# The list scheduler of a transformer layer plays on another simulation of the engines

## The chip, the core and the metric

The kernel runs on one core of a Trainium2 chip. The metric is the device time of one execution, in microseconds (us). Lower is better. The engines are named as the profile names them: PE is TensorE (matmuls; its weight loads are shown apart as PEld), DVE is VectorE, ACT is ScalarE, POOL is GpSimd and SP is SyncE, which here only issues DMAs.

## The reference

One layer of a transformer over 640 tokens of width 1024: 128 context tokens and 512 latent tokens on a grid of 8 rows by 64 columns. All values are fp32. Cut to what matters:

```python
sh1, sc1, g1, sh2, sc2, g2 = split(silu(c) @ w_mod + b_mod, 6)
h = rmsnorm(x, n1) * (1 + sc1) + sh1
aq, ak, av, bq, bk, bv, ga, gb = split(h @ w_in)              # 4352 columns
a_o = softmax attention, 8 query heads on 2 key heads; q and k normalised, 2-D rotary
b_o = neighbourhood attention, 8 heads, window of 8 x 16 grid places, learned bias
x = x + g1 * ((sigmoid(ga) * (a_o @ w_br_a) + sigmoid(gb) * (b_o @ w_br_b)) @ w_out)
h2 = rmsnorm(x, n2) * (1 + sc2) + sh2
x = x + g2 * (square(relu(h2 @ w_mlp_in)) @ w_mlp_out)        # 4096 hidden columns
y = rmsnorm(x, final_g)
```

Latent queries also read 128 cached context keys; context queries read context keys alone. The new keys and values of the context tokens are outputs too.

## The kernel before

**How the work is tiled.** Activations lie transposed, features on the 128 partitions and the 640 tokens along the free axis, in two halves of 320 columns. To keep the precision, each fp32 operand is cut into a high and a low part of the type fp32r: ACT copies the high part and DVE subtracts it to get the low part. Each product is then three matmuls (high by high, high by low, low by high), in `gemm_k` at L320 to L322 and, in the MLP, at L1679 to L1681.

**Its stages.**

1. The start, up to about 48 us: the modulation of the first norm, the first norm and the first three tiles of `w_in`, while the first loads arrive.
2. Attention, about 48 to 320 us. Units of work (`HeadA`, `HeadB`, `CtxPair`) go through scores (`S`: L700 and L701, or L763 and L764), a softmax (DVE maximum L702, ACT exponential L703), transposes (L710, L780), a cut into `ph` and `pl` (ACT L647, DVE L648), and the product with the values (L718 and L722). Between them the generator `fill_tile` gives out the matmuls of the other tiles of `w_in` (`pg`, L320 to L322), so many ns of them between two steps. On the program's side this mix of streams is written out: `attention` calls `F.spend` with what a step has left.
3. Merge, output projection and second norm, about 315 to 510 us. DVE also forms the late part of the modulation there (`wmt` times `cb`, L1123).
4. The MLP, to the end. Its first chunk is plain; from about 557 us on it is computed by a scheme of seven products of half-size blocks (the list `SEQ`, loop at L1665), each into one of eight PSUM banks `b`. Its weights come in as `wst` and `wsb` on SP's queue (L254, L1398). The `wsb` get a second matrix added by a DMA of POOL's queue that accumulates (L1401, L1424). ACT and DVE cut them into `wb` (L1416, L1421), of which six can be alive at once.
5. The tail: the last gated sums (L1532), squares (L1547), the mean by a matmul with ones (L1559), its power -1/2 (L1563, L1564), the final products (L1568) and the stores (L1569).

**What sets the order on the engines.** The Python code traces instructions in program order. When the tracing context closes, a list scheduler plays the program on a simulation of the chip: whenever an engine (or a DMA queue) can take an instruction, it is given the ready one with the best priority, and the priority is the place in program order (a few blocks are moved back or forward with `tc.high_priority(offset=...)`, as the weight cuts in attention by `DEFER` = 60). The order in which the simulation took the instructions becomes the order in each engine's stream. The chip then runs each stream strictly in that order. Buffers of a pool are also handed out at that moment, so which buffer a tile gets follows from the order.

Two stretches are kept in program order by hand. In the start all five engines are:

```python
with tc.manual_schedule(engines={e.engine for e in (PE, ACT, DVE, nc.gpsimd, nc.sync)}):   # L458
```

From the merge to the start of the MLP's first chunk, DVE alone is (L1170 with `MAN = (0,)`, closed at L1638). Everywhere else the simulation decides for all engines and both DMA queues.

## Time and profile before

| | |
|---|---|
| median of 3 runs | 917.35 us (917.27 to 917.84) |
| the profiled execution | 917.51 us, of which 915.7 us from its first to its last instruction |
| busy: PE, PEld | 901.5 us (98%), 871.5 us (95%) |
| busy: DVE, ACT, POOL | 713.5 us (78%), 564.8 us (62%), 197.0 us (22%) |
| bytes moved by DMA | 151.09 MB |
| instructions | 16620 |

A busy time is the sum of the stretches in which an engine ran at least one instruction. A matmul's end in the profile is modelled and matmuls overlap: two of 320 columns start 0.15 us apart in the dense stretches, and each is shown as 0.31 us long. So a PE that is shown busy all the time may still have lost time, which then shows as a longer mean of the matmuls that waited for their operands. Everything in this table but the median is of the one profiled execution.

### The profile page before, as it was taken

Reading aid. Unit: us, or ns where it says so; the run is one execution under the profiler, and the core shown is the slowest. Engines: PE = TensorE matmul, PEld = TensorE weight load, DVE = VectorE, ACT = ScalarE, POOL = GpSimd, SP = SyncE. Lnnn points to the kernel's source line nnn. Section 1 sums busy time; section 2 is a strip of 40 time slices with the busy share of each in tenths; the row PEclk is TensorE's granted clock in tenths of the full one; section 3 lists DMA queues with packets and bytes.
Section 4 is the critical chain, followed back from the end, with each engine's and each line's share of the span. In section 5 each row is a group of like instructions: output and inputs, shape, how many; then the busy total and the mean of one; then the engine's idle time right before and its main releaser. Section 6 shows DMA issues by size and latency. Waiting matters only on the chain.

```text
span 915.7 us, 16620 instructions
## 1 busy us (share of the span) xinstructions
PE 901.5 (98%) x6120; PEld 871.5 (95%) x6120; DVE 713.5 (78%) x1508; ACT 564.8 (62%) x1176; POOL 197.0 (22%) x226
## 2 busy tenths in 40 slices
PE   9999999999999999999999999999999999999996
PEld 7799989999999999999999999999999999999995
DVE  6776887757666796767789996995798769976897
ACT  4566777756667765765325667537753576357765
POOL 0020200001211011211120000354244532454140
PEclk9999999999999999999999999999999999999998
DMA  9892400126645398999743463898778876898475
GB/s 348 317 266 69 113 24 26 62 72 159 161 119 125 120 284 256 249 268 251 251 140 100 116 165 105 134 210 186 186 122 191 178 174 144 180 173 182 97 126 151
DMA packets 54465, 151.09 MB, mean 165 GB/s; under 512 B 6704, under 2 KB 10432, under 8 KB 54384
## 3 DMA queue, kind: packets, MB, share of 16 engines
q1 hardware_dynamic: 31440, 99.74, 33.1%
q0 software_dynamic: 21792, 48.98, 30.8%
q10 hardware_dynamic: 1152, 1.31, 0.4%
q8 instruction: 48, 0.79, 0.4%
q14 instruction: 33, 0.27, 0.1%
HBM read 137.67 MB, written 4.60 MB: 155 GB/s over the span
## 4 chain that ended last, share of the span: by engine, by line
PE 81%; DVE 6%; DMA 5%; ACT 4%; issue 2%; POOL 0%; SPq 0%; DVEq 0%; ACTq 0%; POOLq 0%
PE b L1680 10%; PE b L1679 10%; PE b L1681 10%; PE pg L320 7%; PE pg L321 7%; PE pg L322 7%; PE pss L322 4%; PE pss L321 4%; PE pss L320 4%; DMA wsb<-w 2%; PE pt L321 2%; PE pt L322 2%; PE pt L320 2%; DMA ms<-wmodA 2%; PE pt L710 1%
## 5 line engine op out<-in xcount | busy, mean ns | idle before, releaser
L1416 ACT ACTIVATE wb<-wsb 128x512 fp32r<-128x512 f32 x140 | 87.1, 628 | 90.6 <-PE b L1681 59.2
L1680 PE MATMUL b<-op,wb 128*128 128x320 f32 x448 | 138.6, 309 | 0.7 <-DVE op L1489 0.7
L1679 PE MATMUL b<-op,wb 128*128 128x320 f32 x448 | 138.6, 309 | 0.0
L1681 PE MATMUL b<-op,wb 128*128 128x320 f32 x448 | 138.4, 309 | 0.0
L1421 DVE TENSOR_TENSOR wb<-wsb,wb 128x512 fp32r<-128x512 f32 x124 | 92.5, 749 | 26.5 <-ACT wb L1416 26.3
L1424 POOL DMA_DIRECT2D wsb<-w x84 | 74.4, 922 | 127.8 <-DVE wb L1421 99.7
L1123 DVE SCALAR_TENSOR_TENSOR mt<-wmt,cb 128x512 f32<-128x512 f32 x128 | 80.9, 686 | 6.0 <-DMA wmt<-wmodB 6.0
L1680 PEld LDWEIGHTS b<-op,wb 128*128 128x128 f32 x448 | 84.1, 188 | 1.2 <-DVE op L1489 1.2
L1679 PEld LDWEIGHTS b<-op,wb 128*128 128x128 f32 x448 | 84.1, 188 | 0.5 <-DVE x L1532 0.4
L1681 PEld LDWEIGHTS b<-op,wb 128*128 128x128 f32 x448 | 84.1, 188 | 0.0
L272 ACT ACTIVATE wh<-wst 128x512 fp32r<-128x512 f32 (+1 forms) x84 | 61.1, 739 | 32.1 <-PE pg L321 16.6
L1401 POOL DMA_DIRECT2D wsb<-w x28 | 26.0, 930 | 138.0 <-DVE xm L341 41.5
L281 DVE TENSOR_TENSOR wl<-wst,wh 128x512 fp32r<-128x512 f32 (+1 forms) x53 | 43.3, 821 | 14.9 <-ACT wh L272 12.8
L648 DVE TENSOR_TENSOR pl<-pt,ph 128x512 fp32r<-128x512 f32 (+1 forms) x72 | 44.9, 627 | 11.8 <-ACT ph L647 11.2
L647 ACT ACTIVATE ph<-pt 128x512 fp32r<-128x512 f32 (+1 forms) x72 | 39.2, 548 | 15.7 <-PE po L718 4.7
L1532 DVE SCALAR_TENSOR_TENSOR x<-b,parts,x 128x128 f32<-128x128 f32 (+1 forms) x116 | 46.3, 429 | 2.9 <-PE b L1681 2.2
L1416 ACT ACTIVATE wb<-wst 128x512 fp32r<-128x512 f32 x56 | 34.9, 626 | 17.1 <-PE b L1681 10.3
L1679 PE MATMUL b<-t,wb 128*128 128x320 f32 x144 | 44.7, 310 | 0.0
L1681 PE MATMUL b<-t,wb 128*128 128x320 f32 x144 | 44.5, 309 | 0.0
L1680 PE MATMUL b<-t,wb 128*128 128x320 f32 x144 | 44.5, 309 | 0.0
L1489 DVE TENSOR_TENSOR op<-hid,op 128x1280 fp32r<-128x1280 f32 (+2 forms) x32 | 37.0, 1155 | 7.6 <-ACT op L1488 7.4
L1532 DVE SCALAR_TENSOR_TENSOR x<-tp,parts,x 128x320 f32<-128x320 f32 (+2 forms) x60 | 38.9, 677 | 1.0 <-ACT tp L1583 1.0
(890 smaller groups left out, 3009.2 us busy)
## 6 DMA issues: line engine op xcount, KB each, us to landing
wsb<-w POOLq DMA_DIRECT2D x112, 256.0 KB, 5.1
wst<-w SPq DMA_DIRECT2D x36, 512.0 KB, 3.9
wmt<-wmodB SPq DMA_DIRECT2D x32, 512.0 KB, 5.5
wst<-w_in SPq DMA_DIRECT2D x31, 512.0 KB, 4.4
wsb<-w SPq DMA_DIRECT2D x28, 512.0 KB, 4.0
ms<-wmodA SPq DMA_DIRECT2D x16, 512.0 KB, 8.2
wl<-w_in POOLq DMA_DIRECT2D x10, 512.0 KB, 7.6
wst<-w_br SPq DMA_DIRECT2D x8, 512.0 KB, 4.2
```

Of the source, the lines that this page charges most:

```text
L272: ACT.activation(hi[:, ks], st[:, ks], AF.Copy)
L320: PE.matmul(ps, wh[:, k], xh[:, sl], start=first, stop=False)
L321: PE.matmul(ps, wh[:, k], xl[:, sl], start=False, stop=False)
L322: PE.matmul(ps, wl[:, k], xh[:, sl], start=False, stop=last)
L1123: DVE.scalar_tensor_tensor(t, st[:, q * 512:(q + 1) * 512], 1.0, r32(cb[2 * q + i][:, :512]), op0=OP.mult, op1=OP.mult, accum_out=parts[:, ...
L1416: ACT.activation(w[:, 0:4], t, AF.Copy)
L1421: (nc.gpsimd if o in BLKPOOL[l - 1] else DVE).tensor_sub(w[:, 4:8], t, r32(w[:, 0:4]))
L1424: nc.gpsimd.dma_start(t, self.src(l, c, n, e)[:, 4 * half:4 * half + 4], accum_op=OP.add)
L1532: DVE.scalar_tensor_tensor(X1[i][:, sl], src[:, sl.start - off:sl.stop - off], g[:, j:j + 1], X1[i][:, sl], op0=OP.mult, op1=OP.add)
L1679: PE.matmul(b, w[:, k], xh, start=not whole and k == 0, stop=False, skip_group_check=True)
L1680: PE.matmul(b, w[:, k], xl, start=False, stop=False, skip_group_check=True)
L1681: PE.matmul(b, w[:, 4 + k], xh, start=False, stop=o not in ("A11", "S2", "S1") and k == 3, skip_group_check=True)
```

## The change

One argument of the tracing context. With it, the scheduler plays the program on a simulation that follows the devices of the core one by one: for each engine its sequencer, its queue of issued instructions and the engine itself, the PE's weight loads and matmuls apart, and the DMA queues and engines. Without it, the scheduler uses the library's default simulation, a coarser one. No instruction is added, removed or changed in shape; only orders in the streams, buffers and the semaphore waits that follow from them can differ.

```diff
-    with tile.TileContext(nc) as tc:
+    with tile.TileContext(nc, schedule_with_timeline_sim=True) as tc:
         trunk_layer(tc, *args)
```

## The prediction

> **What bounds the kernel now.** I read the head of the page first, then busy time by stage, then what PE waited for, then the groups of matmuls, then the other engines' waits and the chain that ended last.

> The head of the page says who leads: PE is busy nearly all the span and has most of the chain.

> ```profile
> span 915.7 us, 16620 instructions
> PE 901.5 (98%) x6120; PEld 871.5 (95%) x6120; DVE 713.5 (78%) x1508; ACT 564.8 (62%) x1176; POOL 197.0 (22%) x226
> PE 81%; DVE 6%; DMA 5%; ACT 4%; issue 2%; POOL 0%; SPq 0%; DVEq 0%; ACTq 0%; POOLq 0%
> ```

> The windows by stage (start, attention, merge to second norm, MLP, tail) show where PE lost anything. In each row: the stage, its length, then busy time and count for PE, PEld, DVE, ACT and POOL, the granted clock, the DMA share.

> ```profile
> 0.00:48.00 48.00, 46.22 (x354) 36.38 (x355) 33.20 (x91) 25.32 (x54) 1.74 (x6) 1.00 0.91 331
> 48.00:320.00 272.00, 268.56 (x1799) 252.66 (x1798) 195.45 (x425) 188.30 (x468) 33.94 (x53) 1.00 0.40 108
> 320.00:510.00 190.00, 189.88 (x1289) 188.83 (x1287) 147.46 (x412) 101.50 (x192) 27.24 (x27) 1.00 0.76 221
> 510.00:900.00 390.00, 389.29 (x2640) 387.25 (x2640) 326.76 (x560) 242.29 (x449) 134.06 (x140) 1.00 0.74 157
> 900.00:916.00 16.00, 7.58 (x45) 6.40 (x44) 10.65 (x25) 7.44 (x17) 0.00 (x0) 0.85 0.47 164
> ```

> PE's idle time is 1.78 us in the start, 3.44 in attention, 0.12 from merge to norm, 0.71 in the MLP, and 8.1 in the tail (15.7 - 7.58). So 580 us of the kernel, from 320 to 900, hold 0.83 us of idle PE: no order can gain there, and a bad one can only lose. The number of matmuls does not change.

> Attention's loss is larger than its idle time, since a matmul that waits for its operand is also shown as longer. Compare matmuls of one shape:

> ```profile
> L700 PE MATMUL pss<-kh,qs 128*128 128x320 f32 x64 | 20.1, 321 | 0.1
> L701 PE MATMUL pss<-kl,qs 128*128 128x320 f32 x64 | 19.2, 308 | 0.0
> L718 PE MATMUL po<-ph,vst 128*128 128x512 f32 x40 | 19.0, 478 | 0.8 <-ACT ph L647 0.8
> L722 PE MATMUL po<-pl,vst 128*128 128x512 f32 x40 | 15.4, 408 | 0.1
> L320 PE MATMUL pg<-h0h,wh 128*128 128x320 f32 x44 | 14.9, 339 | 0.9 <-ACT kr L910 0.6 <-DVE vst L640 0.4
> L322 PE MATMUL pg<-h0h,wl 128*128 128x320 f32 x44 | 13.6, 309 | 0.0
> ```

> The first of each pair of lines stands at the place where PE meets a fresh operand. The excess is 64 x 13 ns = 0.8 us (L700), 40 x 70 ns = 2.8 (L718) and 44 x 30 ns = 1.3 (first matmul of a fill half), together 5.0 us. With the 3.44 idle that is 8.4 us of loss to order in 272 us of attention, or 2.45 us of loss for each us shown idle.

> **The change, part by part.** It removes and adds no instruction. What it can move is the order in every stream that is not pinned: PE, ACT, DVE, POOL and the two DMA queues (SP, POOL) from 48 us on, DVE less from the merge to the first chunk of the MLP.

> *The start, 0 to 48 us: 0.* All five engines, SP among them, are in program order there by hand (L458). Its loss is the DMAs' (share 0.91), and they keep their order.

> *Attention, 48 to 320 us.* This is where a list scheduler has most choice: PE can take scores, transposes, value products or fills, and ACT and DVE hold softmax steps of one unit beside weight cuts for a fill much later. I see two opposite effects. A simulation with the real wait between engines knows when `ph` or `pl` is not there yet and puts a fill matmul first: less loss. One that fills each engine's issue queue ahead may put a weight cut, ready early, in front of a softmax step that becomes ready a moment later: more loss. The trace of before shows neither, so I bound it by its own best and worst 40 us:

> ```profile
> 120.00:160.00 40.00, 38.88 (x251) 34.98 (x251) 32.08 (x58) 29.80 (x70) 2.55 (x2) 1.00 0.10 29
> 200.00:240.00 40.00, 39.88 (x281) 38.97 (x280) 27.63 (x77) 27.21 (x75) 7.04 (x14) 1.00 0.55 142
> 240.00:280.00 40.00, 39.79 (x278) 38.26 (x277) 27.71 (x77) 26.63 (x76) 6.67 (x13) 1.00 0.60 151
> ```

> At the worst rate (1.12 idle in 40) the stage has 6.8 x 1.12 = 7.6 idle, times 2.45 = 18.6 us of loss, 10.2 more than now. At the best (0.12) it has 0.8 x 2.45 = 2.0, 6.4 less. No row excludes either sign, so I take the middle, **+1.9 us**, and keep -6.4 and +10.2.

> *Merge to norm and MLP, 320 to 900 us.* What hides order here is reserve: ACT cuts weights as soon as PE gives back a buffer, and the queues wait for the cuts. In the waits (engine and line waited for: us in total, times, longest):

> ```profile
> PE b L1680 <- DVE op L1489: 0.7, 2, 0.4
> ACT wb L1416 <- PE b L1681: 69.5, 77, 1.4
> ACT wb L1416 <- DMA wsb<-w: 22.7, 10, 4.4
> SPq L1398 <- DMA wsb<-w: 126.1, 15, 25.5
> POOL wsb L1424 <- DVE wb L1421: 99.7, 33, 30.9
> ```

> 77 waits of ACT on PE mean that weights are ahead of PE; 10 waits on the accumulated `wsb` mean that sometimes they are not by much. The chain that ended last agrees: it leaves PE for the `wsb` transfer at four places of the MLP, though PE did not idle at them.

> ```profile
> 743.43 5.55 DMA wsb<-w
> 825.82 4.45 DMA wsb<-w
> 831.42 6.90 DMA wsb<-w
> 843.63 4.92 DMA wsb<-w
> ```

> ```profile
> wsb<-w POOLq DMA_DIRECT2D x112, 256.0 KB, 5.1
> ```

> A `wsb` load goes through SP's queue, then POOL's accumulate, then ACT, then DVE, each in its own stream. If the new order puts one accumulate behind a POOL subtraction that waits, or a `wst` load in front of a `wsb` on SP, the product that needs it comes one landing later: 5.1 us if nothing covers it, 0 if the reserve does. Below, the gain is at most the 0.83 us idle. I take a quarter of one landing, **+1.3 us**, for it is nearer to the 0.7 us that PE waits in the whole stretch than to 5.1, and keep -0.8 and +5.1.

> *Tail.* The last product's sum waits on DVE behind final products of the other half (start, us, piece of the chain):

> ```profile
> 904.49 0.46 DVE x L1532
> 904.95 1.20 DVE x L1568 x3
> 906.15 0.47 DVE x L1532
> 906.65 0.48 ACT sq L1547
> 907.17 0.82 PE b L1559 x2
> 908.01 0.53 ACT rstd L1563
> 908.64 0.48 ACT rstd L1564
> 910.03 2.41 DVE x L1568 x6
> ```

> Three L1568 of 0.40 us stand before the L1532 that the end needs. Another order could drop them (-1.2) or put the four others of that half there too (+1.6). I take **0**. The rest of the tail is one dependent chain in any order.

> *Sum.* 0 + 1.9 + 1.3 + 0 = +3.2 us on the profiled execution's 917.51, so 920.7; that execution is 0.16 us above the median of the runs, so **920.6 us**. With the terms at their ends: 917.35 - 6.4 - 0.8 - 1.2 = 909, and 917.35 + 10.2 + 5.1 + 1.6 = 934.

> **The rivals.**

> *Faster: the finer simulation orders attention better.* Its mechanism is the one above: PE takes a fill instead of waiting at L718, L700 and at the first fill matmul. If all of attention came to the rate of 240 to 280 us (0.21 idle in 40), its loss would be 6.8 x 0.21 x 2.45 = 3.5 us, 4.9 less than now: **912.4 us**. For it: the waits are short (the excess of L718 is 70 ns a time), just what a finer clock can see. Against it: fills moved early are missing later, and fills have at most two PSUM banks to run ahead. It decides from 1.8 us recovered in attention, a fifth of its loss. [...]

> *No change: the reserve covers it.* 580 of 916 us have PE full with buffers ahead, 48 are pinned, and attention's two effects may cancel. **917.4 us**, within 1.8 us. That the other simulation yields nearly the same order is a part of this case.

> *Much slower: the MLP's loads come late again and again.* If the order on SP or POOL is worse as a rule and not once, all four places above expose a landing: 4 x 5.1 = 20.4 us, with attention's +1.9: **939.7 us**. For it: SP already waits 126.1 us on `wsb` at L1398. Against it: 77 waits on PE against 10 on loads. It decides once a landing is late by more than PE's reserve. The clock could add to it: after PE's last matmul, at 908 us, the granted clock falls.

> ```profile
> 908.00:911.00 3.00, 0.00 (x0) 0.00 (x0) 2.08 (x6) 1.00 (x2) 0.00 (x0) 1.00 0.76 264
> 911.00:916.00 5.00, 0.00 (x0) 0.00 (x0) 1.45 (x4) 0.00 (x0) 0.00 (x0) 0.51 0.66 227
> ```

> So an idle stretch of PE of 3 us costs nothing more here, and one of over 3 us leads to half a clock. [...]

> **How the numbers follow.** About 0.2% (1.8 us) is what a measurement of this kernel can tell from no change. The forecast (slower by a few us, 919.2 to 934) has 0.38; the much slower case 0.12; the faster one 0.28; no change 0.22. So faster 0.28, same 0.22, slower 0.50. I put the time at 920.6. The range is 909 to 934: below it I leave 0.05 and above it 0.12, most of the much slower case. The forecast's own range is 919.2 to 934. The sign is weakly held: what decides it is that attention can move both ways by about the same, while the stretch from 320 to 900 can only lose.

> **What the profile after would show.** The start's row must repeat (46.2 busy of 48, same pieces). In attention, PE's idle time and the means of L718, L700 and the first fill matmul tell the sign: above 3.44 us and 478 ns for the forecast, below for the faster rival. From merge to MLP, PE's waits should still sum to about 1 to 2 us; a wait at L1679 to L1681 of some us on a `wb` whose `wsb` landed late, and a granted clock under 1.00 before 900 us, would show the much slower case. In the tail, count the L1568 between the last two L1532. The prediction is wrong if attention comes in more than 3 us better, if loads are late more than once, or if the streams of before are kept almost unchanged.

## The result, and the profile after

The changed kernel takes **977.65 us** (median of 4 runs, 975.69 to 979.97), the kernel before 917.6 us beside it: a ratio of 1.065, 95% interval 1.0632 to 1.0669. The prediction said 920.6 us (909 to 934). The likelier sign was right, the size was not: 60 us instead of 3.

The head of the page of the changed kernel (span, busy time, then the chain that ended last):

```profile
span 977.4 us, 16595 instructions
PE 925.7 (95%) x6120; PEld 880.6 (90%) x6120; DVE 705.5 (72%) x1508; ACT 558.5 (57%) x1176; POOL 195.3 (20%) x226
PE 52%; DVE 16%; DMA 14%; ACT 10%; issue 6%; POOL 1%; SPq 0%; DVEq 0%; ACTq 0%; POOLq 0%
```

The five counts of instructions are those of before, so no work was added. But the chain is now on PE for 52% of the span and not for 81%: PE waits for others. Where it does, the windows tell. First before, then after, in the columns of the prediction (stage, length, busy time and count of PE, PEld, DVE, ACT, POOL, granted clock, DMA share, GB/s). The stages are cut where PE starts each: the two halves of attention (A is the global one, `HeadA`, B the neighbourhood one, `HeadB`), then the MLP's first chunk and its scheme of seven products.

```profile
49.00:193.00 144.00, 141.58 (x924) 130.84 (x923) 107.45 (x187) 101.91 (x233) 15.80 (x20) 1.00 0.29 84
193.00:315.00 122.00, 120.98 (x838) 116.21 (x838) 82.45 (x229) 80.41 (x221) 17.97 (x33) 1.00 0.53 138
499.00:557.00 58.00, 57.88 (x390) 56.98 (x389) 51.09 (x105) 35.94 (x77) 3.46 (x4) 1.00 0.43 119
557.00:905.00 348.00, 347.29 (x2358) 345.63 (x2357) 290.79 (x490) 215.46 (x394) 130.60 (x136) 1.00 0.77 159
```

```profile
49.00:204.00 155.00, 146.53 (x929) 130.65 (x928) 109.14 (x188) 102.67 (x234) 14.61 (x19) 1.00 0.28 80
204.00:350.60 146.60, 129.51 (x837) 119.87 (x835) 78.24 (x226) 77.70 (x220) 18.06 (x33) 0.97 0.41 115
536.50:603.70 67.20, 62.73 (x391) 59.98 (x390) 51.50 (x106) 39.08 (x85) 3.48 (x4) 0.95 0.36 108
603.70:966.00 362.30, 352.23 (x2357) 347.03 (x2356) 282.10 (x490) 208.66 (x392) 129.47 (x136) 1.00 0.76 154
```

Nearly the same counts of matmuls (a few fall on the other side of a cut), more idle time and, in two rows, a lower clock. Stage by stage, from PE's first matmul of one stage to its first of the next, before and after, in us of the profiled execution:

| stage | before | after | more |
|---|---|---|---|
| start | 48.9 | 49.5 | 0.6 |
| attention A | 144.2 | 154.4 | 10.2 |
| attention B | 121.7 | 146.7 | 25.0 |
| merge | 127.3 | 128.6 | 1.3 |
| output, second norm | 57.4 | 57.4 | 0.0 |
| MLP, first chunk | 58.0 | 67.1 | 9.1 |
| MLP, seven products | 347.9 | 362.3 | 14.4 |
| tail | 10.3 | 11.4 | 1.1 |

So there are two places to explain: attention, 35.2 us, and the MLP, 23.5 us.

**Attention.** In stage B PE's idle time grew from 1.0 to 17.1 us. Its waits there, before and then after (us in total, times, longest), are these. Before has two and no other:

```profile
PE pg L320 <- DVE vst L640: 0.4, 1, 0.4
PE pt L784 <- DVE pl L648: 0.2, 1, 0.2
```

```profile
PE pss L763 <- DMA kh<-kh: 3.9, 1, 3.9
PE pss L763 <- ACT pc L841: 2.8, 3, 1.1
PE po L805 <- ACT ph L647: 2.6, 2, 1.6
PE po L858 <- DVE bo L655: 2.2, 2, 1.3
```

These are the four largest after. Waits for copied keys come to 4.2 us (0.3 for `kl` beside the 3.9); the other 12.3 us of waits are for ACT and DVE, most of them for steps of the softmax.

The longest single wait ends a chain on one tile. The keys of a new tile of `w_in` are cut into `kh` and `kl`, and DMAs of POOL's queue (L617) copy their halves into a stacked copy, which the scores (L763 for `kh`, L764 for `kl`) read. The chain that ended last shows two copies of `kl`, one after the other (those of `kh` run beside them, the last one issued at 259.07), and the timeline shows PE on both sides of the wait (start, duration, in brackets the idle time and its releaser):

```profile
252.08 0.45 POOL kl L617
252.59 7.96 DMA kl<-kl
260.55 0.28 issue
260.83 5.28 DMA kl<-kl
```

```profile
260.05 0.31 PE L322 MATMUL pg<-h7h,wl 128*128 128x320 f32 x1
...
260.65 0.39 PE L809 MATMUL po<-pl,vst 128*128 128x512 f32 x1
264.90 0.59 PE L763 MATMUL pss<-kh,qs 128*128 128x320 f32 x2 [3.86 <-DMA kh<-kh]
...
266.91 0.47 PE L320 MATMUL pg<-h0h,wh 128*128 128x320 f32 x1
267.17 0.47 PE L321 MATMUL pg<-h0l,wh 128*128 128x320 f32 x1
```

Up to 260.05 PE starts fill matmuls (`pg`, 0.15 us from start to start). Then its stream has the scores next and the next fill behind them (266.91), and PE waits. At 266.91 the matmuls start 0.26 us apart instead of 0.15: the granted clock is 0.50 from 266.90 to 267.50 (more rows on the clock are at the end). How much cover there is can be counted in PE's stream, as matmuls between the last fill of a new key tile and the first scores that read its stacked keys. For the three tiles of stage B these are 145, 142 and 142 before, and 103, 96 and 93 after. At 0.147 us each, 96 matmuls are 14.1 us; from the cut of this tile's keys (249.5) to its last copy's landing (266.1) it took 16.6 us.

Stage A has no wait for a copy. Its idle time grew from 2.4 to 8.5 us, in waits of at most 0.9 us for ACT and DVE.

**MLP.** What PE itself waits for is mostly not weights. In the first chunk it waits 4.2 us for `hh`, the result of the second norm that ACT and DVE cut, and 0.2 for weights. In the seven products it waits 4.0 us for operands that ACT and DVE cut (`op`), 4.7 until they have read a bank (`tp`) and 1.2 for weights. The largest of each stage:

```profile
PE pg L320 <- ACT hh0h L346: 1.5, 1, 1.5
```

```profile
PE b L1679 <- ACT op L1488: 2.7, 3, 1.1
```

In the seven products the chain that ended last goes on from there to the weights: loads into `wsb` are 25.6% of it between 604 and 966 us (6.3% before, between 557 and 905), since ACT cuts weights, cuts operands and reads banks in one stream. The waits of ACT and POOL that the prediction showed for before, now in the changed kernel:

```profile
POOL wsb L1424 <- DVE wb L1421: 145.1, 39, 55.8
ACT wb L1416 <- PE b L1681: 55.5, 52, 2.8
ACT wb L1416 <- DMA wsb<-w: 50.6, 15, 6.1
```

ACT waits for the accumulated `wsb` for 50.6 us and not for 22.7, POOL's accumulating loads wait for DVE's subtractions for 145.1 and not 99.7, and ACT has to wait for PE 52 times and not 77. The reserve of weights is smaller. One piece of the chain shows what such a wait is made of:

```profile
679.36 1.39 POOL wb L1421
680.75 0.49 issue
681.24 0.43 POOL wsb L1401
681.67 0.16 issue
681.83 0.54 POOL wsb L1424
682.37 7.88 DMA wsb<-w
690.33 0.64 ACT wb L1416
```

A subtraction of POOL (L1421, 1.39 us and the issue after it) stands ahead of two accumulating loads. The second load lands 7.88 us later, and ACT's cut starts on its landing. Before had pieces of the same kind (a landing of 5.55 us at 743.43, behind a subtraction of POOL of 1.75 us), but PE did not idle behind them.

### The profile page after: what moved, and what is told of

Its sections match the earlier page's. It is cut to its first block, busy times and chain, and to the rows that moved or that the text cites. A ratio compares the mean times of both kernels' runs of the same rounds, so it can differ in the third digit from the quotient of the medians.

```text
span 977.4 us, 16595 instructions
## 1 busy us (share of the span) xinstructions
PE 925.7 (95%) x6120; PEld 880.6 (90%) x6120; DVE 705.5 (72%) x1508; ACT 558.5 (57%) x1176; POOL 195.3 (20%) x226
## 4 chain that ended last, share of the span: by engine, by line
PE 52%; DVE 16%; DMA 14%; ACT 10%; issue 6%; POOL 1%; SPq 0%; DVEq 0%; ACTq 0%; POOLq 0%
DMA wsb<-w 9%; PE pg L320 6%; PE pg L321 6%; PE pg L322 6%; DVE wb L1421 4%; PE pss L321 4%; PE pss L322 3%; PE pss L320 3%; DVE x L1532 3%; PE b L1679 2%; PE b L1681 2%; PE b L1680 2%; PE pt L320 2%; PE pt L321 2%; PE pt L322 2%
## 5 line engine op out<-in xcount | busy, mean ns | idle before, releaser
L1416 ACT ACTIVATE wb<-wsb 128x512 fp32r<-128x512 f32 x140 | 85.7, 626 | 106.9 <-DMA wsb<-w 50.6
L1679 PE MATMUL b<-op,wb 128*128 128x320 f32 x448 | 135.9, 312 | 5.5 <-ACT op L1488 2.7
L1680 PE MATMUL b<-op,wb 128*128 128x320 f32 x448 | 138.3, 310 | 1.3 <-DVE op L1489 1.3
L1681 PE MATMUL b<-op,wb 128*128 128x320 f32 x448 | 136.0, 310 | 0.0
L1421 DVE TENSOR_TENSOR wb<-wsb,wb 128x512 fp32r<-128x512 f32 x124 | 91.5, 750 | 42.9 <-ACT wb L1416 42.9
L1424 POOL DMA_DIRECT2D wsb<-w x84 | 76.0, 966 | 152.7 <-DVE wb L1421 145.1
L1679 PEld LDWEIGHTS b<-op,wb 128*128 128x128 f32 x448 | 83.1, 188 | 7.9 <-ACT op L1488 3.5
L1680 PEld LDWEIGHTS b<-op,wb 128*128 128x128 f32 x448 | 84.3, 188 | 2.2 <-DVE op L1489 2.1
L272 ACT ACTIVATE wh<-wst 128x512 fp32r<-128x512 f32 (+1 forms) x84 | 58.8, 737 | 47.2 <-PE pg L321 21.9
L1681 PEld LDWEIGHTS b<-op,wb 128*128 128x128 f32 x448 | 83.8, 188 | 0.0
L647 ACT ACTIVATE ph<-pt 128x512 fp32r<-128x512 f32 (+1 forms) x72 | 39.9, 558 | 15.3 <-PE pt L710 6.1
L1489 DVE TENSOR_TENSOR op<-hid,op 128x1280 fp32r<-128x1280 f32 (+2 forms) x32 | 37.9, 1184 | 14.3 <-ACT op L1488 14.3
L1532 DVE SCALAR_TENSOR_TENSOR x<-b,parts,x 128x128 f32<-128x128 f32 (+2 forms) x116 | 46.5, 432 | 0.1
L1681 PE MATMUL b<-t,wb 128*128 128x320 f32 x144 | 44.6, 310 | 0.4 <-DVE wb L1421 0.2
L1679 PE MATMUL b<-t,wb 128*128 128x320 f32 x144 | 44.5, 310 | 0.4 <-DVE tp L1518 0.4
L1680 PE MATMUL b<-t,wb 128*128 128x320 f32 x144 | 44.4, 309 | 0.0
L1416 ACT ACTIVATE wb<-wst 128x512 fp32r<-128x512 f32 x56 | 34.7, 624 | 13.9 <-PE b L1681 10.6
L1421 DVE TENSOR_TENSOR wb<-wst,wb 128x512 fp32r<-128x512 f32 x44 | 32.6, 745 | 11.4 <-ACT wb L1416 10.7
## 6 DMA issues: line engine op xcount, KB each, us to landing
wsb<-w POOLq DMA_DIRECT2D x112, 256.0 KB, 5.6
```

The costliest lines, as they stand in the source:

```text
L272: ACT.activation(hi[:, ks], st[:, ks], AF.Copy)
L1416: ACT.activation(w[:, 0:4], t, AF.Copy)
L1421: (nc.gpsimd if o in BLKPOOL[l - 1] else DVE).tensor_sub(w[:, 4:8], t, r32(w[:, 0:4]))
L1424: nc.gpsimd.dma_start(t, self.src(l, c, n, e)[:, 4 * half:4 * half + 4], accum_op=OP.add)
L1532: DVE.scalar_tensor_tensor(X1[i][:, sl], src[:, sl.start - off:sl.stop - off], g[:, j:j + 1], X1[i][:, sl], op0=OP.mult, op1=OP.add)
L1679: PE.matmul(b, w[:, k], xh, start=not whole and k == 0, stop=False, skip_group_check=True)
```

## The experiments

Two edits are used. **A pinned order**: the program is traced once with the default context, and each engine's order is read from it. It is then traced again with the changed context, and neighbours in that order are tied for the named engines, in a stretch of the program or in all of it. The ties bind the scheduler and put no wait on the chip (with all five streams tied the time is 918.26 us, beside 918.22 for the kernel before); engines that are not named are planned anew around them. Cut to what matters:

```python
def pin(engines, stretch):                 # at: instruction by name
    for e in engines:
        for a, b in zip(order[e], order[e][1:]):   # inside the stretch
            tc.add_manual_dep(at[b], a, NoSync, ...)
```

**The depth of the simulated issue queues.** In the library's finer simulation an instruction is taken when it enters the simulated issue queue of its engine. Its place in the stream is fixed there, ahead of its execution; work that becomes ready in between comes behind it, whatever its priority. The depth is a setting of that simulation, and `full` below holds its defaults; what the chip itself holds, no run shows.

```python
full = dict(spec.ENG_ISSUE_QUEUE_DEPTH)
spec.ENG_ISSUE_QUEUE_DEPTH = full | {E.PE: 12}     # the context runs with this
```

Stage times of all runs, in us, of the profiled execution (start, output and tail are left out: in every run each is within 1.5 us of before):

| kernel | A | B | merge | chunk 0 | seven products | whole, median |
|---|---|---|---|---|---|---|
| before | 144.2 | 121.7 | 127.3 | 58.0 | 347.9 | 917.6 to 918.6 |
| after | 154.4 | 146.7 | 128.6 | 67.1 | 362.3 | 977.65 |
| e1 all five pinned | 144.2 | 121.7 | 128.1 | 58.0 | 347.0 | 918.26 |
| e2 PE pinned | 156.8 | 128.1 | 127.1 | 64.1 | 360.0 | 957.17 |
| e3 ACT, DVE pinned | 163.8 | 144.8 | 131.5 | 61.2 | 364.9 | 985.5 |
| e4 SP, POOL pinned | 153.8 | 152.4 | 128.6 | 67.1 | 355.0 | 976.8 |
| e5 PE's queue 12 | 146.4 | 124.8 | 128.3 | 65.3 | 359.0 | 943.08 |
| e6 PE's queue 4 | 145.5 | 124.3 | 128.8 | 62.2 | 359.3 | 940.86 |
| e7 all queues 2 | 146.8 | 122.9 | 128.6 | 61.7 | 357.1 | 937.14 |
| e8 PE default, others 1 | 153.1 | 140.6 | 130.2 | 66.4 | 357.5 | 968.32 |
| e9 = e7 + PE in MLP | 146.8 | 122.8 | 129.6 | 63.6 | 359.7 | 941.31 |
| e10 = e7 + ACT, DVE in MLP | 145.4 | 124.4 | 128.3 | 60.7 | 352.8 | 930.55 |
| e11 = e7 + SP, POOL in MLP | 147.0 | 122.9 | 129.6 | 61.7 | 350.1 | 930.45 |
| e12 default, PE's B stream new | 144.2 | 138.2 | 127.7 | 58.0 | 346.3 | 936.92 |
| e13 = e7 + all but PE in MLP | 146.3 | 124.4 | 129.5 | 60.7 | 348.0 | 927.64 |
| e14 = e7 + POOL in MLP | 146.2 | 124.5 | 128.0 | 61.7 | 350.8 | 929.98 |
| e15 = e7 + SP in MLP | 145.9 | 122.9 | 128.3 | 61.7 | 352.9 | 937.36 |

**Is it order, or buffers and waits?** The context is the changed one, all five streams are pinned.

```diff
+    pin(("PE", "ACT", "DVE", "POOL", "SP"), whole)
```

> The scheduler plays on the finer simulation, but the streams of all five engines are pinned to the order that the default simulation gave, so that only buffers and waits can differ. If the 60 us come from order (the theory), the time is 917.6 us within 0.3%. If they come from the buffers that were handed out otherwise (a rival), it stays at 960 us or more.

918.26 us, ratio 0.9999 (0.9984 to 1.0013). In the traces PE, ACT, DVE and POOL run the same instruction at every place as before. Order makes all of it; the buffers that the other simulation hands out for that order make nothing that can be measured.

**Which engine's order?** One group pinned at a time.

```diff
+    pin(("PE",), whole)                   # e2
+    pin(("ACT", "DVE"), whole)            # e3
+    pin(("SP", "POOL"), whole)            # e4
```

> The finer simulation, with the PE stream alone pinned to the order of the default simulation; ACT, DVE, POOL and SP are free. Theory: PE's own order is the cause, since it puts matmuls closer behind what they wait for (93 to 103 matmuls instead of 142 to 145 between a new key tile and its first scores). Then most of the 60 us are gone: 915 to 930 us. Rival (ACT and DVE have the wrong order, and PE only follows): at least half stays, 945 us or more.

> The finer simulation, with the ACT and DVE streams pinned to the order of the default simulation; PE and the DMA queues are free. Theory (PE's order is the cause): PE still has only 103 to 112 matmuls between a new key tile and its first scores, so it still waits, somewhat less: 940 to 970 us. Rival (ACT and DVE): back to 915 to 930 us.

> The finer simulation, with the streams of SP and POOL (all DMA queues of the kernel but ACT's stores) pinned to the order of the default simulation; PE, ACT and DVE are free. Theory (PE's order): no gain, 970 to 985 us. Rival (loads and accumulating loads were put in a worse order, the much slower case of the prediction): 935 us or less.

957.17, 985.5 and 976.8 us (ratios 1.0421, 1.0756, 1.0647). PE's order, pinned alone, brings stage B from 146.7 to 128.1, but stage A gets longer (156.8). With ACT and DVE in the order of before, A is longer still (163.8). In both, the simulation plans the free engines anew around the pinned ones, and in A that comes out worse than either plan as a whole. That was not expected, and pins over the whole program could not separate the causes. The queues' order saves 7.3 us in the seven products and nothing in attention, which is 5.1 us longer.

**Is it the depth of the queue in the simulation?** No order of before is used here.

```diff
+    spec.ENG_ISSUE_QUEUE_DEPTH = full | {E.PE: 12}                  # e5
+    spec.ENG_ISSUE_QUEUE_DEPTH = full | {E.PE: 4}                   # e6
+    spec.ENG_ISSUE_QUEUE_DEPTH = {e: 2 for e in full}               # e7
+    spec.ENG_ISSUE_QUEUE_DEPTH = full | {e: 1 for e in full if e != E.PE}  # e8
```

> [...] Rival (the simulated latencies are wrong, whatever the depth): stays over 960 us.

> [...] Theory: the choice is made 0.6 us ahead at most, and most of the loss goes: 918 to 935 us; the stream has 141 to 145 matmuls again between a new key tile and its first scores. Rival (latencies): over 960 us.

> The finer simulation with all five queues at 2 places. Theory: nearly the order of an immediate choice, 912 to 925 us; if the finer simulation's better latencies are worth anything, this is where it shows, at or below 917 us. Rival (latencies): over 960 us.

> [...] Theory (PE's depth): little is gained, 955 to 985 us. [...]

943.08, 940.86, 937.14 and 968.32 us (ratios 1.0264, 1.0238, 1.0189, 1.0555). The first lies in the 930 to 950 us that were expected if choosing ahead is the cause. Attention follows PE's depth: 301.1 us at the default, 271.2 at 12, 269.8 at 4, 269.7 with all at 2, against 265.9 before. With PE at its default and all others at 1 it is 293.7, so the other queues have a part too, of up to 7.4 us. The cover of the three key tiles moves with it: 145, 141, 141 matmuls at 4 and at 2, 104, 103, 101 with PE at its default and the others at 1. At 12, though, two of the three are 112, and stage B is as short (124.8) as at 4: the count of matmuls tells whether cover is short, not by how many us. The whole came out above what was expected at 4 and 2, for the MLP gave back less than attention. What in the finer simulation makes the rest of the loss, once its queues are short, no run tests; its latencies are one candidate.

**Does PE's order make stage B long?** The kernel before, with the default simulation, and only PE's stream in stage B pinned to the order of the changed kernel.

```diff
-    with tile.TileContext(nc, schedule_with_timeline_sim=True) as tc:
+    with tile.TileContext(nc) as tc:      # order: from the finer simulation
+    pin(("PE",), "mixer B")
```

> One part of the change alone: the default simulation everywhere, but PE's stream in the second half of attention (from the start of mixer B to the merge) pinned to the order that the finer simulation gave, with 93 to 103 matmuls between a new key tile and its first scores. Theory (PE meets keys that are still being copied): the stage takes 135 to 147 us in place of 121.7, and the kernel 931 to 943 us. Rival (it was ACT's and DVE's order in that stage): 925 us or less.

936.92 us, ratio 1.0189 (1.0137 to 1.0242). The window of stage B and PE's waits:

```profile
193.00:332.00 139.00, 127.76 (x840) 120.15 (x840) 82.64 (x229) 78.74 (x219) 17.96 (x33) 0.98 0.45 121
```

```profile
PE pss L763 <- ACT pb L771: 4.2, 4, 2.0
PE pss L763 <- ACT pc L841: 2.9, 3, 1.1
PE pss L764 <- DMA kl<-kl: 2.2, 3, 1.3
```

Stage B is 16.5 us longer, 16.5 of the 25.0, in the shortest of four executions (933.2 to 947.55 us). So PE's order is enough for most of the stage's loss. It is not the only order that differs, though: the default simulation planned the other engines around it, and ACT and DVE each hold another instruction than before at 179 places, most of them in this stage. What PE's order would cost with theirs held, no run shows. The waits are of the kinds of the changed kernel: scores before their stacked keys (2.7 us of the 11.2 idle, with 0.5 for `kh`), and above all scores before ACT has given back the bank that its exponential reads (7.1). All other stages are as before, to 1.6 us.

**What is left in the MLP with short queues?** All queues at 2 leave the MLP (both rows) at 418.8 us, 12.9 above before. From there, orders of before in the MLP alone. Three executions that have the order of before in the whole MLP (before, e1, e12) took 405.9, 405.0 and 404.3 us there, so differences of 1 to 2 us tell nothing.

```diff
     spec.ENG_ISSUE_QUEUE_DEPTH = {e: 2 for e in full}
+    pin(("PE",), "mlp")                          # e9
+    pin(("ACT", "DVE"), "mlp")                   # e10
+    pin(("SP", "POOL"), "mlp")                   # e11
+    pin(("ACT", "DVE", "SP", "POOL"), "mlp")     # e13
+    pin(("POOL",), "mlp")                        # e14
+    pin(("SP",), "mlp")                          # e15
```

> All queues at 2 places as in e7_all_depth2 (937 us; its MLP, from its first matmul to the last product, takes 418.8 us against 405.9 before). From the MLP's start on, PE's stream is pinned to the default simulation's order. If PE's own order makes the 13 us there: 922 to 928 us. If ACT and DVE or the loads do: 934 us or more.

> As e9_mlp_pe, with the ACT and DVE streams pinned from the MLP's start on in place of PE's. If the order of weight cuts, operand cuts and sums on ACT and DVE makes the 13 us: 922 to 928 us. If PE's order or the loads do: 934 us or more.

> As e9_mlp_pe, with the SP and POOL streams pinned from the MLP's start on in place of PE's. If the order of the loads and accumulating loads makes the 13 us: 922 to 928 us. If PE, ACT or DVE do: 934 us or more.

> The issue queues of the finer simulation at 2 places, and from the MLP on the orders of ACT, DVE, POOL and SP as in the kernel before; PE's order there stays the finer simulation's. Theory (the MLP's rest of 13 us is the order of the loads and of the work of ACT and DVE that frees their buffers, the two add up, PE's own order costs nothing): MLP of 406 to 410 us against 418.8 with the depth alone and 405.9 before, whole 921 to 926 us. Rival (PE's order in the MLP also has to fit the others', as in the first attention stage): MLP of 414 or more, whole 931 or more.

> As with all issue queues at 2 places, but from the MLP on POOL's order alone is that of the kernel before. Theory (the loads that add to the weight sums stand behind POOL's subtractions): MLP of 411 to 414 us, whole 928 to 932 us, as with POOL and SP together. Rival (it is SP's loads that are ordered later): MLP of 417 to 420 us, whole 935 to 939 us.

> As with all issue queues at 2 places, but from the MLP on SP's order alone is that of the kernel before. Theory (POOL's order is the queues' cost): MLP of 417 to 420 us, whole 935 to 939 us. Rival (SP's loads are the cost): MLP of 411 to 414 us, whole 928 to 932 us.

941.31, 930.55, 930.45, 927.64, 929.98 and 937.36 us (ratios 1.0247, 1.0132, 1.0133, 1.0104 with 1.0089 to 1.012, 1.0127, 1.0228). MLP of the profiled executions: 423.3, 413.5, 411.8, 408.7, 412.5 and 414.6 us. PE's own order saves nothing. POOL's alone gives what both queues give (6.3 and 7.0 us), and ACT's and DVE's 5.3; together (e13) they give 10.1, less than the sum by 2 us, which is no more than the scatter. Both e10 and e11 lie between what was expected if their order made all of the 13 us and if it made none. SP's order gives nothing by the medians (937.36 beside 937.14). Its profiled execution took 930.56 us, the shortest of five from 930.56 to 940.28, so its stage time isn't typical. The whole of e13 is 1.6 us above what was expected: the MLP is in its bounds, and the rest of the distance to before lies in attention (4.8) and the merge (2.2).

What is different in POOL's stream can be read in one place of the two programs. Left as in the kernel before (and e14), right with all queues at 2:

```
L1421 TENSOR_TENSOR wb<-wsb,wb        L1421 TENSOR_TENSOR wb<-wsb,wb
L1424 DMA wsb<-w                      L1421 TENSOR_TENSOR wb<-wst,wb
L1421 TENSOR_TENSOR wb<-wst,wb        L1424 DMA wsb<-w x3
L1424 DMA wsb<-w                      L1421 TENSOR_TENSOR wb<-wst,wb
L1421 TENSOR_TENSOR wb<-wst,wb        L1424 DMA wsb<-w x2
L1424 DMA wsb<-w x2
```

Three loads stand behind a second subtraction there, and POOL's subtractions wait for ACT's cuts (with all queues at 2, L1421 on L1416: 19.2 us in 10 waits). ACT's waits for `wsb` from the MLP's start (all at 2, then POOL's order of before, then four orders of before):

```profile
ACT wb L1416 <- DMA wsb<-w: 42.3, 17, 5.4
```

```profile
ACT wb L1416 <- DMA wsb<-w: 29.5, 13, 5.5
```

```profile
ACT wb L1416 <- DMA wsb<-w: 24.4, 14, 5.8
```

With four orders the wait is near the 22.7 us of before, and PE in the seven products has 1.4 us of idle time left, not 7.8 as in e7, where it waited 4.1 us for weights (length less PE's busy time; e13 first, then e7):

```profile
567.40:915.50 348.10, 346.70 (x2358) 345.56 (x2357) 290.27 (x490) 214.25 (x393) 130.74 (x136) 1.00 0.78 159
```

```profile
567.60:924.70 357.10, 349.32 (x2358) 345.79 (x2357) 287.01 (x488) 214.06 (x394) 130.79 (x136) 1.00 0.76 155
```

So of the MLP's 23.5 us, 10.6 go with the queues' depth (429.4 to 418.8), 10.1 with the order of the four streams beside PE's at 2 places, and 2.8 stay open; nearly all of these (2.7) are in the first chunk, which took 58.0 us in all three executions with the order of before. No stage of any run is shorter than before by more than the scatter.

## Why the prediction was wrong

- **The start: 0.** Held: 0.6 us, and 48.7 us with every stream pinned.
- **Attention: +1.9, at most +10.2; measured +35.2.** This is the step that failed. I bounded a new plan by the best and worst 40 us of the old plan's trace. Those rows show how far one plan varies within itself; they do not bound another. The effect was named ("One that fills each engine's issue queue ahead may put a weight cut, ready early, in front of a softmax step"), but I saw it on ACT and DVE, as a moment's delay of a softmax step. The runs show it on PE above all: with its simulated queue at the default depth fills are spent early, and the scores of stage B come 40 to 50 matmuls sooner after the fills of their keys. With that queue at 4 places, 31.3 of the 35.2 us are gone. That the early fills also cause the many short waits for ACT and DVE, the larger part of PE's idle time, fits this but was not separated; no single wait of stage A was followed up. The old trace held a number that would have warned me of the copies: the stacking copies (`kh<-kh`, `kl<-kl`) land after 4.5 us by the median and 8.0 at most, and some go one after the other. In stage B of before PE waited for none of them, with 142 to 145 matmuls between; in the changed kernel, with 93 to 103, its waits for them come to 4.2 us. The view of line 617 in before shows it:

```profile
DMA to landing us min/median/max: 2.7/4.5/8.0
```

- **The signs to look for.** Idle time in attention above 3.44 us: yes, 25.6 (302.60 less 277.03 from 48 to 350.6 us). L700 above 321 ns: yes, 333, and the first fill matmul is up from 343 to 358 in attention. L718 above 478: no, it fell to 444, while the idle time ahead of it rose from 0.8 to 1.9 us, so a part of its waiting may stand there now. A mean duration of a shape alone is then a poor measure. So is the factor 2.45: 25.6 times 2.45 would be 62.7 us of loss, and the measured loss is 35.2 + 8.4 = 43.6. Of the signs for the much slower case, a clock under 1.00 before 900 us came, but not PE's waits of some us on a late `wb`: there are two, 1.2 us in all.

```profile
48.00:350.60 302.60, 277.03 (x1771) 251.51 (x1769) 188.16 (x415) 181.37 (x456) 32.67 (x52) 0.98 0.35 98
...
L700 PE MATMUL pss<-kh,qs 128*128 128x320 f32 x64 | 20.8, 333 | 1.0 <-ACT pa L703 0.8
L718 PE MATMUL po<-ph,vst 128*128 128x512 f32 x40 | 17.4, 444 | 1.9 <-ACT ph L647 1.1 <-DVE ao L655 0.8
```

- **Merge to MLP: +1.3, at most +5.1; measured +24.8.** "One accumulate behind a POOL subtraction that waits" is what happens, and POOL's order is worth 6.3 us, above the end that I gave it. What was mis-sized is how often: I priced one landing, and ACT's waits for `wsb` grew from 22.7 to 50.6 us. I also gave no price to two other parts, ACT's and DVE's order (5.3 us) and the first chunk (9.1 us), which had 0.12 us of idle PE before. There it is not the weights: PE waits for `hh`, and three windows of 4 us at a clock of 0.77, 0.50 and 0.87 lack another 3.4 us at most. That "no order can gain there, and a bad one can only lose" held. I then took the loss to be small because the old plan's waits were small.
- **The tail: 0, at most +1.6; measured +1.1.** In its bounds, and by the step that I gave to the upper end: eight L1568 stand ahead of the last L1532, where four stood.
- **The rivals.** "Faster" fails at its point of decision: attention recovered nothing. "The streams stay nearly the same" fails too. "Much slower" (939.7) had the right side and, for the MLP, the right place: 4 landings of 5.1 us are 20.4, and 23.5 was measured. That these are near each other is luck: 9.1 of the 23.5 are in the first chunk, where this case had nothing, POOL's order makes only a part, and attention was the larger half of the whole.

## What to carry to other kernels

A plan's own trace does not bound another plan. When the order of everything can change, find what the present order hides (a transfer of 5 to 8 us behind fills, loads behind a queue's own arithmetic, each softmax step behind other matmuls) and price it exposed, as often as it occurs. Before trusting a finer simulation as a scheduler, ask at which moment it fixes the order: here, fixing it when an instruction enters a queue of the default depth spent filler work early (attention 301.1 us, and 269.8 with 4 places on PE). Taking one engine's order from another plan can be worse than either plan.

## What the runs showed of the hardware

```profile
264.00:268.00 4.00, 2.95 (x13) 2.60 (x14) 1.14 (x4) 0.39 (x1) 0.00 (x0) 0.71 0.12 25
...
812.00:816.00 4.00, 4.00 (x17) 3.60 (x17) 2.19 (x4) 2.66 (x6) 0.00 (x0) 0.59 0.53 126
```

Ahead of 542 us the longest wait is 1.39 us, but PE started only 10 matmuls in 4 us, against 27 at its dense rate (0.147 us from start to start):

```profile
538.00:540.00 2.00, 0.61 (x3) 0.19 (x1) 1.01 (x6) 1.83 (x4) 0.00 (x0) 1.00 0.02 4
540.00:542.00 2.00, 1.40 (x7) 0.84 (x6) 2.00 (x10) 1.14 (x4) 0.00 (x0) 1.00 0.00 0
542.00:544.00 2.00, 1.72 (x6) 1.39 (x6) 2.00 (x5) 0.49 (x2) 0.00 (x0) 0.55 0.00 0
```

Behind the wait of 3.86 us that ends at 264.90 the clock is 0.50 from 266 to 268 us; behind the stretch at 538 us, thin but with no long wait, it is 0.55 from 542 to 544. So a stretch of few matmuls was paid twice here. The runs show no threshold for it: from 558 to 562 us PE started 12 matmuls and was busy for 1.99 us, against 10 and 2.01 us from 538 to 542, and the clock stayed at 1.00.

```profile
558.00:560.00 2.00, 0.64 (x5) 0.38 (x3) 1.43 (x4) 1.79 (x6) 1.38 (x2) 1.00 1.03 422
560.00:562.00 2.00, 1.35 (x7) 1.10 (x8) 2.00 (x6) 1.89 (x5) 1.58 (x2) 1.00 1.14 202
562.00:564.00 2.00, 2.00 (x16) 2.00 (x15) 2.00 (x5) 0.56 (x1) 0.15 (x1) 1.00 1.00 174
```

Over the ten windows, the share of the clock missing gives 23.7 us at half the clock, so at most 11.8 of the 60 us are the clock's (an estimate: part of that time PE had nothing to run).

A second thing is the spread. Five executions of e15 lie 9.7 us apart and four of e12 14.4, each with one fixed order. It is not a mark of slow plans as such: four of e5 lie 1.5 us apart, ten of e1, with the order of before, 6.2. Of the kernel before, seven lie 2.1 us apart on e15's chip, and on e12's chip six lie 6.0 apart while a seventh took 3490.07 us. The cause of the spread is not shown.
